# A hybrid decoder layer on one core: order of the splits ahead of the feed-forward block, place of one product in its streams, and the last pair's sums kept in SBUF

## The chip, the core and the metric

The kernel runs on one core of a Trainium2 chip. The metric is the device time in microseconds of one execution; the median of three runs is given. TensorE's clock is told by the granted clock of the profile: 1.00 is 2.4 GHz, 0.50 is 1.2 GHz.

## The reference

One decoder layer over 1024 tokens of width 1024, in float32. The part that matters here is its end:

```python
x = x + gate1 * jnp.dot(merged, w_out)
h2 = _rmsnorm(x, norm2_w) * (1.0 + scale2) + shift2
ffn = jnp.dot(jax.nn.silu(jnp.dot(h2, w_ffn_gate)) * jnp.dot(h2, w_ffn_up), w_ffn_down)
x = x + gate2 * ffn
return _rmsnorm(x, final_norm_w)
```

The hidden width of the feed-forward block is 2816, which is 22 blocks of 128 columns.

## The kernel before

**Splits.** Every factor of a matrix product is stored as two tiles, hi and lo: ScalarE copies the source into hi in a rounded format (fp32r), VectorE or GpSimd subtracts hi from the source into lo. A product is then three matmuls, hi by hi, hi by lo and lo by hi, and each is 128x512 here.

**Products.** The gate and up matrices are taken in pairs of 128-column blocks. There are 11 pairs; each pair has two streams, first gate, then up, so 22 streams. In a stream a two-by-two block product of h2 (transposed) and the weights is made out of seven products M1 to M7 with sums of blocks as factors (a Strassen-like scheme). Each product is 12 matmuls (four blocks of the contraction by three). Their sides that come from h2 lie in SBUF as "combos": h11 for M1, S1 for M5, S2 for M6, S4 for M3, S3 for M7, h21 for M2, h22 for M4. The weight sides are made new for each stream by `factor`: a difference on VectorE (L789, L795, L796), the hi on ScalarE and the lo on `lo_engine` (L750, L751), into five slots `fhi` and `flo`. M1, M6, M7 and M4 of a stream add up in one PSUM bank ("ya", four of them): after M1 and M6 ScalarE copies what is there (L807), after M7 VectorE adds it to a tile (L810), and M4 is the last in the bank. M5 and M3 share a bank of "yb" (two of them); M2 has one for itself.

**The way in.** The last stage before, x plus the gated output projection, goes tile by tile of 128 tokens in the order 4, 5, 6, 7, 0, 1, 2, 3. For each it makes the norm, transposes the normed tile on TensorE (L1377), scales the transposed blocks on ScalarE and VectorE (L1383, L1387) into `hraw`, and puts the part of the combos that this tile gives (`put_half1`, `put_half2`, `put_rest`, with `put_combo` at L1277 and L1278 for hi and lo). So the combos h11 (M1's) and h21 (M2's) are whole only when the last tile, number 3, is split. The M5 products of the first four streams need nothing of the last tiles; they stand in between, to keep TensorE busy. The rest of the combos, S2, S4 and S3, are sums and splits (`split_combo` at L1502 and L1503, sums at L1295, L1301 and L1536). Until the ninth product of the first pair VectorE makes the weights' lo halves too, afterwards GpSimd does.

**The way out.** Silu of the gate stream's four blocks (L1428) times the up stream's (L1431) gives the activations, and four sums of them follow (L1455 to L1458). Seven tiles of each pair are stored in DRAM (`act_d`, L1446). The rows of the down matrix that belong to the pair are loaded (L1473), four sums are made of them in place in one buffer `dw` (L1485), and stored in DRAM (`dw_d`, L1496). After the last pair the down projection runs in six passes (M1, M5, M6, M3, M7, M4), each over all 11 pairs, and a seventh (M2) with the final norm. Its factors are loaded again (L1583) through a ring of eight raw tiles, split (L1586 and L1587) and multiplied (L1604 to L1606).

**Order.** All instructions are written down in one order by hand, and a planner, which knows each instruction's dependencies and estimates its cost, sets from that the fixed order of each engine's queue: of what it holds ready it takes what was written first. Each engine then works its queue strictly in order. `turns_after(a, b)` tells the planner to put a behind b on the same engine without a wait at run time. DMAs all go through SyncE's queue.

Of the kernel before, what the change touches and what calls it, by code (L numbers as in the profile page):

```python
# [43 lines left out]
def tile_hybrid_layer(ctx: ExitStack, tc: tile.TileContext, x, c, w_ada, b_ada, norm1_w, w_in,  # L44
# [704 lines left out]
    def split_block(src, hi, lo, eng=None):  # L749
        ins = nc.scalar.activation(hi, src, AF.Copy)  # L750
        (eng or nc.gpsimd).tensor_sub(lo, src, f32(hi))  # L751
        return ins

    class Stream:
# [28 lines left out]
        def factor(self, m):  # L783
            b = self.blocks
            if m in ("M1", "M2", "M3"):
                src = b[{"M1": "11", "M2": "21", "M3": "22"}[m]]
            elif m == "M4":
                src = self.t2
                nc.vector.tensor_sub(src, b["21"], src)  # L789
            else:  # L790
                src = four(self.env.tmp())
                x, y = {"M5": ("12", "11"), "M6": ("22", None), "M7": ("22", "12")}[m]
                if m == "M6" and "M5" in self.early:
                    self.t1 = src
                    nc.vector.tensor_sub(src, b["12"], b["11"])  # L795
                nc.vector.tensor_sub(src, b[x], b[y] if y else self.t1)  # L796
                if m == "M5":
                    self.t1 = src
                if m == "M6":
                    self.t2 = src  # L800
            hi, lo = self.env.slot()
            self.split = split_block(src, hi, lo, self.env.lo_engine)
            return hi, lo
# [69 lines left out]
    class GateEnv:  # L873
# [20 lines left out]
        def quad(self, *_):  # L894
            self.n_q += 1
            return quads[(self.n_q - 1) % len(quads)]

        def store(self, st, dst, src):
# [376 lines left out]
    def put_combo(name, o, src):  # L1275
        hi, lo = (c[:, :, o:o + P] for c in combo[name])
        nc.scalar.activation(hi, src, AF.Copy)  # L1277
        nc.vector.tensor_sub(lo, src, f32(hi))  # L1278

# [11 lines left out]
    def put_half1(o):  # L1291

        h11, h21, h12, s1 = parts_of(o)
        put_combo("h11", o, h11)
        nc.vector.tensor_sub(s1, s1, h11)  # L1295

    def put_rest(o):

        h11, h21, h12, s2 = parts_of(o)
        put_combo("h21", o, h21)  # L1300
        nc.vector.tensor_sub(h21, h21, s2)  # L1301

    raws = []
# [27 lines left out]
    for hf in range(2):  # L1331
# [16 lines left out]
        for n, t in enumerate(order):  # L1348
# [23 lines left out]
            for g in range(2):  # L1372
# [5 lines left out]
                for i in range(4):  # L1378
# [7 lines left out]
                    else:  # L1386
                        nc.vector.tensor_scalar(h_to, h_of, sc, sh, op0=ALU.mult, op1=ALU.add)  # L1387
            (put_half2 if th else put_half1)(o)
    alloc_combo("h21")
    for i in range(4):  # L1390
        put_rest(i * P)
    st_f.close()
# [12 lines left out]
    class FfnEnv:  # L1405
        lo_engine = nc.vector

        def __init__(self):
# [38 lines left out]

    todo = []

    def finish_tasks(p):  # L1450

        g, u = streams[p, 0], streams[p, 1]
        a = g.c
        s1, s2, s3, s4 = u.c["11"], u.c["12"], u.c["22"], quad_tile("s4")
        todo.append(lambda: nc.vector.tensor_add(s1, a["21"], a["22"]))  # L1455
        todo.append(lambda: nc.vector.tensor_sub(s2, s1, a["11"]))
        todo.append(lambda: nc.vector.tensor_sub(s3, a["11"], a["21"]))
        todo.append(lambda: nc.vector.tensor_sub(s4, a["12"], s2))  # L1458
        for m, t in (("M1", a["11"]), ("M2", a["12"]), ("M4", a["22"]), ("M5", s1), ("M6", s2), ("M7", s3),
                     ("M3", s4)):  # L1460
            todo.append(lambda m=m, t=t: act_store(p, m, t))
        if p:
            down_load(p - 1)
        if p > 1:
            down_sums(p - 2)
# [13 lines left out]
    def down_sums(p):  # L1479
# [15 lines left out]
        step(b21, b21, b22)  # L1495
        todo.insert(4, lambda: nc.sync.dma_start(out=dw_d[p], in_=dws[p]))  # L1496

    def split_combo(name, srcs):
        alloc_combo(name)
        for k in range(4):  # L1500
            hi, lo = (c[:, k, :] for c in combo[name])
            nc.scalar.activation(hi, srcs[:, k, :], AF.Copy)  # L1502
            nc.vector.tensor_sub(lo, srcs[:, k, :], f32(hi))  # L1503

# [12 lines left out]
    for st in flow[:2]:  # L1517
        st.prepare("M1")
        turns_after(scaled[3], st.split)
    s3 = ffn.tile([P, 4, H], F32, name="s3", tag="dw")  # L1520
    held2 = const.tile([P, 2, H], F32, name="held2", tag="gate")

    for st, after in zip(flow, (None, {0: 2}, {2: 3}, {0: 3})):
        st.product("M5", after)
        if st.p == 0:
            turns_after(scaled[3], st.copied)
    split_combo("S2", hraw[1][:, 1])
    seq = [(st, m) for m in ("M1", "M2", "M4", "M6", "M3", "M7") for st in flow[:2]]
    n_first = len(seq)
    seq += [(st, m) for st in flow[2:] for m in ORDER if m not in st.early]  # L1530

    def behind(i):
        st, m = seq[i]
        if i == 0:
            for k in range(4):
                nc.vector.tensor_sub(s3[:, k, :], hraw[0][:, 0, k, :], hraw[1][:, 0, k, :])  # L1536
        if i == 1:
            split_combo("S4", hraw[0][:, 1])
        if i == 3:
            split_combo("S3", s3)  # L1540
        if i == 8:
            fenv.lo_engine = nc.gpsimd
        if i == 9:
            flow[2].open()
# [34 lines left out]
    def down_slot(src, lo_eng, scale=None):  # L1579
# [34 lines left out]

    ss3 = {}

    def square(t, i, c0, c1):
        if t not in ss3:
            ss3[t] = const.tile([P, 16], F32, name="ss3", bufs=4)
        sq = ffn.tile([P, H], BF16, name="sqh", tag="quad", bufs=10)  # L1620
        nc.scalar.activation(sq[:, :c1 - c0], x1[t][:, c0:c1], AF.Square, accum_out=ss3[t][:, i:i + 1])

    def final_norm(t, n_parts):
# [8 lines left out]
        nc.sync.dma_start(out=out[t * P:(t + 1) * P, H:], in_=xo[1])  # L1632
        nc.vector.scalar_tensor_tensor(xo[0], x1[t][:, :H], rs, fnorm[:, :H], op0=ALU.mult, op1=ALU.mult)
        nc.sync.dma_start(out=out[t * P:(t + 1) * P, :H], in_=xo[0])

    def second_half(t):
        square(t, 0, H, 2 * H)
        nc.gpsimd.tensor_mul(xo_all[:, (2 * t + 1) % 8, :], x1[t][:, H:], fnorm[:, H:])

# [99 lines left out]
```

## Time and profile before

| what | us |
|---|---|
| median of 3 runs (1787.62 to 1791.78) | 1787.7 |
| the profiled execution, its own time | 1787.85 |
| span in the profile, first to last instruction | 1785.9 |
| busy: TensorE, VectorE, GpSimd, ScalarE | 1701.2, 1228.8, 888.6, 754.3 |
| mean granted clock of TensorE | 0.989 |

The profile records each instruction of each engine with its start and length. A wait is the idle time of an engine ahead of an instruction, and the releaser is the instruction that ended it. Matmuls are pipelined, so that one that is listed with 0.39 us is followed by the next after some 0.23 us.

### The profile page before, as it was taken

What the parts mean: (1) busy time and instruction counts of PE and PEld (TensorE: products, weight loads), DVE (VectorE), ACT (ScalarE), POOL (GpSimd) and SP (SyncE); (2) the same over time, 40 slices, a digit from 0 to 9 for tenths busy, and PEclk for the clock granted to TensorE, in tenths of its full rate; (3) what the DMA queues carried; (4) which work ended last, traced back from release to release, by engine and by line L of the source; (5) the groups of instructions that cost most, each with busy time, mean ns of one, the idle gap of its engine ahead of it and who ended that gap; (6) DMA issues with size and microseconds to landing.
All of it is one profiled execution on the core that took longest, in us unless ns stands there. A gap on an engine that the chain in (4) does not pass through costs nothing. (4 is left out here: it accounts for less than half of the span.)

```text
span 1785.9 us, 24646 instructions
## 1 busy us (share of the span) xinstructions
PE 1701.2 (95%) x8266; PEld 1397.1 (78%) x8266; DVE 1228.8 (69%) x2089; ACT 754.3 (42%) x1469; POOL 888.6 (50%) x883
## 2 busy tenths in 40 slices
PE   5898989999989999999999999899999999999998
PEld 4797868787867888788777888688787878787887
DVE  7528789999699246469876656865656555686665
ACT  3625632342444344430477246533333333444444
POOL 4562275582665479530246640044444444556664
PEclk9999999999999999999999999999999999999999
DMA  9534552411423355865852740034445444597663
GB/s 291 147 108 144 159 161 54 148 33 51 127 77 112 116 156 186 257 203 161 193 128 72 249 162 1 30 118 159 144 151 178 147 137 147 187 311 259 212 185 109
DMA packets 182655, 266.49 MB, mean 149 GB/s; under 512 B 13872, under 2 KB 111616, under 8 KB 180096
## 3 DMA queue, kind: packets, MB, share of 16 engines
q1 hardware_dynamic: 182528, 264.91, 47.4%
q8 instruction: 65, 1.06, 0.2%
q14 instruction: 62, 0.51, 0.1%
HBM read 195.39 MB, written 69.47 MB: 148 GB/s over the span
## 5 line engine op out<-in xcount | busy, mean ns | idle before, releaser
L80 POOL TENSOR_TENSOR wlo<-wraw,whi 128x512 fp32r<-128x512 f32 (+2 forms) x116 | 144.7, 1261 | 111.4 <-ACT whi L77 101.0
L464 DVE TENSOR_SCALAR_CACHE_REDUCE eq<-score,cand 128x384 uint8<-128x384 f32 (+2 forms) x192 | 180.8, 942 | 4.5
L751 POOL TENSOR_TENSOR flo<-tmp,fhi 128x512 fp32r<-128x512 f32 x79 | 106.3, 1346 | 141.1 <-ACT fhi L750 77.0
L121 PE MATMUL mm<-whi,hT_hi 128*128 128x512 f32 (+1 forms) x432 | 160.2, 376 | 3.6 <-ACT qk L644 1.8
L123 PE MATMUL mm<-wlo,hT_hi 128*128 128x512 f32 (+1 forms) x432 | 161.5, 376 | 0.0
L124 PE MATMUL mm<-whi,hT_lo 128*128 128x512 f32 (+1 forms) x432 | 161.2, 376 | 0.0
L827 PE MATMUL ya<-hc,fhi 128*128 128x512 f32 x344 | 134.7, 392 | 2.3 <-DVE c L810 1.4
L1587 DVE TENSOR_TENSOR dslot<-draw,dslot 128x512 fp32r<-128x512 f32 x88 | 96.1, 1127 | 55.3 <-ACT dslot L1586 48.1
L829 PE MATMUL ya<-hc,fhi 128*128 128x512 f32 x344 | 134.1, 390 | 0.0
L1586 ACT ACTIVATE dslot<-draw 128x512 fp32r<-128x512 f32 x154 | 90.1, 626 | 102.1 <-DMA draw<-dw_d 22.8
L831 PE MATMUL ya<-hc,flo 128*128 128x512 f32 x344 | 132.5, 390 | 0.0
L1587 POOL TENSOR_TENSOR dslot<-draw,dslot 128x512 fp32r<-128x512 f32 x66 | 98.7, 1508 | 63.5 <-ACT dslot L1586 60.4
L751 POOL TENSOR_TENSOR flo<-raws,fhi 128x512 fp32r<-128x512 f32 x60 | 82.1, 1368 | 92.5 <-ACT fhi L750 64.3
L77 ACT ACTIVATE whi<-wraw 128x512 fp32r<-128x512 f32 (+2 forms) x116 | 67.0, 590 | 116.6 <-DMA wraw<-in_w_in_dram 48.4
L829 PE MATMUL yb<-hc,fhi 128*128 128x512 f32 x256 | 101.0, 395 | 6.1 <-DVE hc L1278 6.1
L831 PE MATMUL yb<-hc,flo 128*128 128x512 f32 x256 | 101.1, 395 | 3.2 <-POOL flo L751 3.2
L827 PE MATMUL yb<-hc,fhi 128*128 128x512 f32 x256 | 100.8, 395 | 0.6 <-DVE c L810 0.4
L750 ACT ACTIVATE fhi<-tmp 128x512 fp32r<-128x512 f32 x84 | 53.0, 631 | 113.3 <-PE ya L829 60.3
L751 POOL TENSOR_TENSOR wlo<-wraw,whi 128x512 fp32r<-128x512 f32 x52 | 80.5, 1556 | 35.1 <-ACT whi L750 33.3
L121 PEld LDWEIGHTS mm<-whi,hT_hi 128*128 128x128 f32 x432 | 81.2, 189 | 15.9 <-ACT qk L644 2.2
L1127 POOL TENSOR_SCALAR sx<-sx,mx 128x128 f32<-128x128 f32 (+7 forms) x64 | 47.5, 748 | 91.0 <-DVE mx L1126 69.4
L124 PEld LDWEIGHTS mm<-whi,hT_lo 128*128 128x128 f32 x432 | 81.7, 190 | 12.6 <-issue 0.5
(408 smaller groups left out, 4935.9 us busy)
## 6 DMA issues: line engine op xcount, KB each, us to landing
draw<-act_d SPq DMA_DIRECT2D x77, 256.0 KB
mw<-in_w_ada_dram SPq DMA_DIRECT2D x32, 512.0 KB
act_d<-c SPq DMA_DIRECT2D x64, 256.0 KB
raw<-in_w_in_dram SPq DMA_DIRECT2D x26, 512.0 KB
raws<-in_w_ffn_gate_dram SPq DMA_DIRECT2D x24, 512.0 KB
raws<-in_w_ffn_up_dram SPq DMA_DIRECT2D x24, 512.0 KB
dw<-in_w_ffn_down_dram SPq DMA_DIRECT2D x22, 512.0 KB
dw_d<-dw SPq DMA_DIRECT2D x11, 1024.0 KB
```

What stands on the lines that cost most here:

```text
L77: ins = nc.scalar.activation(hi[:, :n], raw[:, :n], AF.Copy)
L80: nc.gpsimd.tensor_sub(lo[:, :n], raw[:, :n], f32(hi[:, :n]))
L121: ins = nc.tensor.matmul(ps, lhsT=ahi, rhs=whi[:, :n], start=(i == 0), stop=False)
L123: nc.tensor.matmul(ps, lhsT=ahi, rhs=wlo[:, :n], start=False, stop=False)
L124: nc.tensor.matmul(ps, lhsT=alo, rhs=whi[:, :n], start=False, stop=(i == last))
L464: ins = [nc.vector.tensor_scalar(eq[:, :sc.shape[1]], sc, thr[j], None, op0=op, op1=ALU.add, accum_out=cnt[:, j:j + 1]) for j, sc in enume ...
L751: (eng or nc.gpsimd).tensor_sub(lo, src, f32(hi))
L827: mm = nc.tensor.matmul(ps, lhsT=whi[:, k, :], rhs=hhi[:, k, :], start=own and k == 0, stop=False, skip_group_check=True)
L829: nc.tensor.matmul(ps, lhsT=whi[:, k, :], rhs=hlo[:, k, :], start=False, stop=False, skip_group_check=True)
L831: nc.tensor.matmul(ps, lhsT=wlo[:, k, :], rhs=hhi[:, k, :], start=False, stop=k == 3, skip_group_check=True)
L1586: nc.scalar.activation(slot[:, 0], raw, AF.Copy)
L1587: lo_eng.tensor_sub(slot[:, 1], raw, f32(slot[:, 0]))
```

## The change

Three edits. First, `put_half1` and `put_rest` return the two splits of the last tile, and a new function `in_turn` puts behind them, on ScalarE and VectorE, all later weight splits, weight differences, sums and combo splits of the first products; M1's own lo halves stand ahead of h11's. One group of M5's matmuls of the fourth stream may also stand ahead of tile 3's transposes (the group that has to wait is now the second of four instead of the first). Second, from the second pair on M4 of a stream is written down behind M1 of the next stream instead of ahead of it. Third, the last pair's seven activation tiles and four sums of down rows are no longer stored and loaded again: the down passes split them from where they lie in SBUF. For that the final norm's weights, which shared a buffer with those sums, go into two tiles of their own ("quad"), and the squares of the final norm share one tile.

```diff
     def split_block(src, hi, lo, eng=None):
         ins = nc.scalar.activation(hi, src, AF.Copy)
-        (eng or nc.gpsimd).tensor_sub(lo, src, f32(hi))
-        return ins
+        return ins, (eng or nc.gpsimd).tensor_sub(lo, src, f32(hi))
...
                 if m == "M6" and "M5" in self.early:
                     self.t1 = src
-                    nc.vector.tensor_sub(src, b["12"], b["11"])
-                nc.vector.tensor_sub(src, b[x], b[y] if y else self.t1)
+                    self.env.in_turn(None, nc.vector.tensor_sub(src, b["12"], b["11"]))
+                self.env.in_turn(None, nc.vector.tensor_sub(src, b[x], b[y] if y else self.t1))
...
-            self.split = split_block(src, hi, lo, self.env.lo_engine)
+            self.split, self.lo = split_block(src, hi, lo, self.env.lo_engine)
+            self.env.in_turn(self.split, self.lo)
...
-        put_combo("h11", o, h11)
-        nc.vector.tensor_sub(s1, s1, h11)
+        ins = put_combo("h11", o, h11)
+        turns_after(nc.vector.tensor_sub(s1, s1, h11), ins[1])
+        return ins
...
-            (put_half2 if th else put_half1)(o)
+            last_h11 = (put_half2 if th else put_half1)(o)
     alloc_combo("h21")
     for i in range(4):
-        put_rest(i * P)
+        last_h21 = put_rest(i * P)
...
     class FfnEnv:
         lo_engine = nc.vector
+        behind = []
+
+        def in_turn(self, scalar, vector):
+
+            for hi, lo in self.behind:
+                if scalar is not None:
+                    turns_after(scalar, hi)
+                turns_after(vector, lo)
...
-            todo.append(lambda m=m, t=t: act_store(p, m, t))
+            if p < NP - 1:
+                todo.append(lambda m=m, t=t: act_store(p, m, t))
+            else:
+                last_act[m] = t
...
-        todo.insert(4, lambda: nc.sync.dma_start(out=dw_d[p], in_=dws[p]))
+        if p < NP - 1:
+            todo.insert(4, lambda: nc.sync.dma_start(out=dw_d[p], in_=dws[p]))
...
         turns_after(scaled[3], st.split)
+        turns_after(last_h11[1], st.lo)
+    fenv.behind = [last_h11, last_h21]
...
-    for st, after in zip(flow, (None, {0: 2}, {2: 3}, {0: 3})):
+    for st, after in zip(flow, (None, {0: 2}, {2: 3}, {1: 3})):
         st.product("M5", after)
         if st.p == 0:
             turns_after(scaled[3], st.copied)
+        else:
+            turns_after(st.copied, last_h11[0])
...
+    for i in [i for i, (st, m) in enumerate(seq[:-1]) if m == "M4" and i >= n_first]:
+        seq[i:i + 2] = seq[i + 1], seq[i]
...
-        if i == 0:
+        if i == 1:
+            fenv.behind += [(f.split, f.lo) for f in flow[:2]]
             for k in range(4):
-                nc.vector.tensor_sub(s3[:, k, :], hraw[0][:, 0, k, :], hraw[1][:, 0, k, :])
-        if i == 1:
+                fenv.in_turn(None, nc.vector.tensor_sub(s3[:, k, :], hraw[0][:, 0, k, :], hraw[1][:, 0, k, :]))
             split_combo("S4", hraw[0][:, 1])
...
-    fnorm = ffn.tile([P, 4, H], F32, name="fnorm", tag="dw")[:, 0:2, :].rearrange("p a n -> p (a n)")
-    nc.sync.dma_start(out=fnorm, in_=final_norm_w.rearrange("(o d) -> o d", o=1).partition_broadcast(P))
-    nc.gpsimd.tensor_scalar(fnorm, fnorm, float(D ** 0.5), 1.0, op0=ALU.mult, op1=ALU.mult)
+    fnorm = [quad_tile("fnorm") for _ in range(2)]
+    for hf, fn in enumerate(fnorm):
+        nc.sync.dma_start(out=fn, in_=final_norm_w[hf * H:(hf + 1) * H].rearrange("(o d) -> o d", o=1)
+                          .partition_broadcast(P))
+        nc.gpsimd.tensor_scalar(fn, fn, float(D ** 0.5), 1.0, op0=ALU.mult, op1=ALU.mult)
...
-        raw, slot = raw_ring[:, n % 8, :], slot_rings[n // 4 % 6][:, n % 4]
-        nc.sync.dma_start(out=raw, in_=src)
+        raw, slot = src if here else raw_ring[:, n % 8, :], slot_rings[n // 4 % 6][:, n % 4]
+        if not here:
+            nc.sync.dma_start(out=raw, in_=src)
...
-        s = down_slot(act_d[p][:, ACT_AT[m], :], nc.vector)
+        here = p == NP - 1
+        s = down_slot(last_act[m] if here else act_d[p][:, ACT_AT[m], :], nc.vector, here=here)
         if m in DW_AT:
+            if here:
+                return s, down_slot(dws[p][:, DW_AT[m], :], nc.gpsimd, here=True)
             src = dw_d[p][:, DW_AT[m], :]
```

## Rows read from the trace of the kernel before

**Rows 1.** The waits of TensorE from 1000 us on: who waited for whom, us, times, longest
```profile
PE yb L829 <- DVE hc L1278: 6.1, 1, 6.1
PE yb L1604 <- ACT dslot L1586: 3.3, 1, 3.3
PE yb L831 <- POOL flo L751: 3.2, 4, 0.8
PE ya L827 <- DVE c L810: 1.4, 4, 0.3
PE ty L1377 <- DVE xn L1374: 1.0, 1, 1.0
PE ya L827 <- ACT c L807: 1.0, 4, 0.2
```

**Rows 2.** Busy time by engine in the two long waits and behind each, with the granted clock
```profile
core 0: us, PE busy (x) PEld busy (x) DVE busy (x) ACT busy (x) POOL busy (x), PEclk, DMA share, GB/s
1137.00:1143.30 6.30, 0.27 (x2) 0.00 (x0) 6.30 (x12) 2.82 (x6) 0.00 (x0) 0.87 0.52 166
1143.30:1148.50 5.20, 5.16 (x12) 4.10 (x13) 5.04 (x9) 0.91 (x2) 0.00 (x0) 0.50 0.00 0
1622.90:1626.40 3.50, 0.23 (x2) 0.02 (x1) 0.00 (x0) 0.70 (x2) 1.93 (x2) 1.00 1.03 379
1626.40:1629.90 3.50, 3.50 (x9) 2.79 (x10) 2.82 (x2) 2.01 (x4) 3.49 (x3) 0.52 0.56 178
```

**Rows 3.** The timeline of VectorE around the first wait: start, length, instruction
```profile
1132.29 1.37 DVE L1387 TENSOR_SCALAR hraw<-ty,modr 128x128 f32<-128x128 f32 x4 [0.26 <-PE ty L1377]
...
1142.61 1.28 DVE L1278 TENSOR_TENSOR hc<-hraw,hc 128x512 fp32r<-128x512 f32 x2
```

**Rows 4.** Busy time by engine between the last scaling and the two splits
```profile
1133.60:1142.60 9.00, 3.67 (x17) 2.70 (x15) 9.00 (x16) 5.24 (x11) 0.00 (x0) 0.95 0.37 117
```

**Rows 5.** The timeline of ScalarE in the same stretch
```profile
1128.75 1.14 ACT L750 ACTIVATE fhi<-raws 128x512 fp32r<-128x512 f32 x2
...
1131.86 1.50 ACT L1383 ACTIVATE hraw<-ty,modr 128x128 f32<-128x128 f32 x4 [1.00 <-PE ty L1377]
...
1134.76 1.16 ACT L1277 ACTIVATE hc<-hraw 128x512 fp32r<-128x512 f32 x2
```

**Rows 6.** The timeline of TensorE ahead of the first wait
```profile
1136.20 0.61 PE L827 MATMUL yb<-hc,fhi 128*128 128x512 f32 x2
```

**Rows 7.** GpSimd by line, 1130 to 1170 us
```profile
L751 POOL TENSOR_TENSOR flo<-tmp,fhi 128x512 fp32r<-128x512 f32 x1 | 1.3, 1297 | 36.2 <-PE ya L829 36.2
```

**Rows 8.** The sums for down by the tile's view: ns, shortest, median and longest
```profile
L1485 DVE TENSOR_TENSOR dw<-dw x44: 676/693/1810, 1239.1 to 1612.3; 128x512 f32<-128x512 f32 x44
```

**Rows 9.** ScalarE's timeline at one boundary of two streams
```profile
1288.56 0.58 ACT L807 ACTIVATE c<-ya 128x512 f32<-128x512 f32 x1
...
1291.29 0.58 ACT L807 ACTIVATE c<-yb 128x512 f32<-128x512 f32 x1
```

**Rows 10.** VectorE's and TensorE's timeline at the same boundary
```profile
1290.50 0.67 DVE L810 TENSOR_TENSOR c<-c,ya 128x512 f32<-128x512 f32 x1
...
1291.23 0.50 PE L827 MATMUL ya<-hc,fhi 128*128 128x512 f32 x1 [0.35 <-DVE c L810]
```

**Rows 11.** The chain that ended last, ahead of the second wait: start, us, what
```profile
1609.13 0.69 DVE dw L1485
...
1612.29 0.70 DVE dw L1485
...
1613.01 5.80 DMA dw_d<-dw
...
1619.21 6.46 DMA draw<-dw_d
...
1625.70 0.64 ACT dslot L1586
```

More of the change, by code (lines that the diff above doesn't have):

```diff
@@ L896, in quad, with in_turn @@
             return quads[(self.n_q - 1) % len(quads)]
+        def in_turn(self, *_):
+            pass
         def store(self, st, dst, src):
@@ L1276, in put_combo @@
         hi, lo = (c[:, :, o:o + P] for c in combo[name])
-        nc.scalar.activation(hi, src, AF.Copy)
-        nc.vector.tensor_sub(lo, src, f32(hi))
+        ins = nc.scalar.activation(hi, src, AF.Copy)
+        return ins, nc.vector.tensor_sub(lo, src, f32(hi))
     def parts_of(o):
@@ L1293, in put_half1 @@
         h11, h21, h12, s1 = parts_of(o)
-        put_combo("h11", o, h11)
-        nc.vector.tensor_sub(s1, s1, h11)
+        ins = put_combo("h11", o, h11)
+        turns_after(nc.vector.tensor_sub(s1, s1, h11), ins[1])
+        return ins
     def put_rest(o):
         h11, h21, h12, s2 = parts_of(o)
-        put_combo("h21", o, h21)
+        ins = put_combo("h21", o, h21)
         nc.vector.tensor_sub(h21, h21, s2)
+        return ins
     raws = []
@@ L1448, in tile_hybrid_layer @@
     todo = []
+    last_act = {}
     def finish_tasks(p):
@@ L1501, in split_combo @@
             hi, lo = (c[:, k, :] for c in combo[name])
-            nc.scalar.activation(hi, srcs[:, k, :], AF.Copy)
-            nc.vector.tensor_sub(lo, srcs[:, k, :], f32(hi))
+            fenv.in_turn(nc.scalar.activation(hi, srcs[:, k, :], AF.Copy),
+                         nc.vector.tensor_sub(lo, srcs[:, k, :], f32(hi)))
     tmps = [tmp_tile() for _ in range(2)]
@@ L1542, in behind @@
             fenv.lo_engine = nc.gpsimd
+            fenv.behind = []
         if i == 9:
@@ L1573, in tile_hybrid_layer, with down_slot @@
     n_slot = [0]
-    fnorm = ffn.tile([P, 4, H], F32, name="fnorm", tag="dw")[:, 0:2, :].rearrange("p a n -> p (a n)")
-    nc.sync.dma_start(out=fnorm, in_=final_norm_w.rearrange("(o d) -> o d", o=1).partition_broadcast(P))
-    nc.gpsimd.tensor_scalar(fnorm, fnorm, float(D ** 0.5), 1.0, op0=ALU.mult, op1=ALU.mult)
+    fnorm = [quad_tile("fnorm") for _ in range(2)]
[3 more added lines that the diff above has]
+        nc.gpsimd.tensor_scalar(fn, fn, float(D ** 0.5), 1.0, op0=ALU.mult, op1=ALU.mult)
     xo_all = slab_tile(7, [P, 8, H], F32, "xo")
-    def down_slot(src, lo_eng, scale=None):
+    def down_slot(src, lo_eng, scale=None, here=False):
         n = n_slot[0]
         n_slot[0] += 1
-        raw, slot = raw_ring[:, n % 8, :], slot_rings[n // 4 % 6][:, n % 4]
-        nc.sync.dma_start(out=raw, in_=src)
+        raw, slot = src if here else raw_ring[:, n % 8, :], slot_rings[n // 4 % 6][:, n % 4]
+        if not here:
+            nc.sync.dma_start(out=raw, in_=src)
         if scale is not None:
@@ L1613, in add_out @@
         nc.vector.tensor_add(x1[t][:, cs], x1[t][:, cs], d)
-    ss3 = {}
+    ss3, squares = {}, []
     def square(t, i, c0, c1):
@@ L1619, in square @@
             ss3[t] = const.tile([P, 16], F32, name="ss3", bufs=4)
-        sq = ffn.tile([P, H], BF16, name="sqh", tag="quad", bufs=10)
+        if not squares:
+            squares.append(ffn.tile([P, H], BF16, name="sqh", tag="quad", bufs=10))
+        sq = squares[0]
         nc.scalar.activation(sq[:, :c1 - c0], x1[t][:, c0:c1], AF.Square, accum_out=ss3[t][:, i:i + 1])
@@ L1632, in final_norm @@
         nc.sync.dma_start(out=out[t * P:(t + 1) * P, H:], in_=xo[1])
-        nc.vector.scalar_tensor_tensor(xo[0], x1[t][:, :H], rs, fnorm[:, :H], op0=ALU.mult, op1=ALU.mult)
+        nc.vector.scalar_tensor_tensor(xo[0], x1[t][:, :H], rs, fnorm[0], op0=ALU.mult, op1=ALU.mult)
         nc.sync.dma_start(out=out[t * P:(t + 1) * P, :H], in_=xo[0])
@@ L1637, in second_half @@
         square(t, 0, H, 2 * H)
-        nc.gpsimd.tensor_mul(xo_all[:, (2 * t + 1) % 8, :], x1[t][:, H:], fnorm[:, H:])
+        nc.gpsimd.tensor_mul(xo_all[:, (2 * t + 1) % 8, :], x1[t][:, H:], fnorm[1])
     banks = {"A": [ps_a() for _ in range(4)], "B": [ps_b(), ps_b(), ps_ty(), ps_ty()]}
```

## The prediction

> **What bounds the kernel now.** I read the page first: TensorE is busy 1701.2 of 1785.9 us, so what can be won is where TensorE waits, and what its clock loses behind a wait. Then I read its waits from 1000 us on, where all three edits lie [rows 1]. They are of three kinds. One long wait, 6.1 us, for a lo half of a combo (L1278). One of 3.3 us, in the down passes, for a split (L1586). And twelve short ones in the streams: four for GpSimd's lo half (3.2 us together), four for VectorE's add (1.4 us), four for ScalarE's copy (1.0 us). The windows on the long waits [rows 2] show a second cost: behind the first the granted clock is 0.50 for 5.2 us, behind the second 0.52 for 3.5 us, so that matmuls take twice as long there; elsewhere around them it is 1.00.
>
> Who is to blame for the first wait is seen on VectorE. The last scaling of tile 3 begins at 1132.29 and lasts to 1133.66, and the two lo halves that TensorE waits for begin only at 1142.61 [rows 3]. ScalarE had the two hi halves ready at 1135.92 (1134.76 plus 1.16) [rows 5]. In between VectorE is busy all 9.0 us, with 16 instructions in the window of which the first is the scaling's end [rows 4]; the other 15 are weight differences, sums and weight lo halves for later products. So it is a matter of order alone.
>
> The second wait is read from the chain of work that ended last [rows 11]: the last pair's four sums on VectorE (1609.13 to 1612.99), their store to DRAM (5.80 us), the load of one of them back (6.46 us), its split on ScalarE at 1625.70, then TensorE.
>
> **The splits first.** The change puts 13 of the 15 instructions behind the two lo halves; the other two are M1's own lo halves, which must stay ahead. Each takes 9.0 / 15 = 0.60 us from start to start [rows 4]. Latest case: VectorE ends the scaling at 1133.66, makes M1's two lo halves to 1134.9 (their hi halves are ready from 1129.89 [rows 5]), then h11's to 1135.5 and h21's to 1136.1. ScalarE ends its scaling at 1133.36 [rows 5] and can give h11's hi half at about 1134.0 (0.58 us, half of the 1.16 for two), h21's at 1134.5, both before VectorE asks. TensorE is busy with M5 until 1136.20, where in this trace it begins the products of h11 and h21 [rows 6]. So both halves come just in time, M5 being the cover. The wait of 6.1 us goes, and with it the slow clock behind it: twelve matmuls in the 5.2 us window [rows 2] took 0.43 us apiece instead of 0.23, which makes 2.4 us. Term: -8.5 us. Bounds: -7.0 (h11's lo half 1.5 us late, as two or three instructions more in front of it would make it) and -8.7 (half of the 5.2 us instead of 2.4).
>
> The group of M5 that may go ahead of the transposes can fill part of the 1.0 us that TensorE waits there for the normed tile [rows 1]: three matmuls of 0.23 us, 0.7 us at most, nothing if the queue stays as it is, and it ends the cover earlier by as much. Term: -0.3.
>
> Then the 13 instructions come later, and what is late next is what they feed: M6's and M4's weight factors, S2, S4 and S3. TensorE goes through M1 and M2 of both streams first, 48 matmuls at 0.23 us, 10.9 us, to about 1147.1. Until then VectorE, at 0.60 us apiece from 1136.1, can make 18 instructions: the weight lo halves of M2 (two), the differences (four), S2's last sum and four lo halves, M6's first lo half, that is 12, so that six others may come between. From there each product gives it 2.7 us, or four to five instructions, and needs two to four. It is enough, with 2 to 4 us to spare, but the queue is a planner's. Term: +1.0; bounds 0 and +4 (half of the 13 x 0.60 = 7.8 us).
>
> **M4 behind the next M1.** At a boundary of two streams, ScalarE has copied the next stream's M1 ("c<-ya") at 1288.56 [rows 9], and M4 of the stream before begins at 1291.23, when VectorE's add to the tile of M7 has been made at 1290.50 [rows 10]. So in TensorE's queue M4 already stands behind the next M1, even behind its M5: the planner had found nothing else ready. Writing it down so changes the queue little. What it can move is who comes first to a free slot or tile: M1's factor and copy then go ahead of M4's. Four of the short waits are M6 waiting for just that copy. The bounds are the short waits: all of them, 5.6 us idle and 0.1 us to start again for each of 12 (a first matmul of 0.50 us instead of 0.39 [rows 10]), 6.8 us won; or as much again lost, if the new order brings as many more. I take a value nearer to nothing: -1.5.
>
> **The last pair on chip.** Store and load go away, 12.3 us of the chain [rows 11]; what remains is sums, split on ScalarE (0.64 us) and GpSimd's lo half (1.3 us as in [rows 7]). If VectorE ends the sums at 1612.99 as before, the factor is there at about 1615, and TensorE needs it at 1622.9 [rows 2]. So the wait of 3.3 us goes, and the slow clock behind it: 3.5 us at 0.52 are 1.7 us lost. The load that sat in this raw tile also held the next load for the same tile; that one comes earlier, too, and with eleven tiles fewer to load the transfers have room, at a DMA share of 1.03 in the wait [rows 2]. Term: -5.0; bounds -5.0 and -3.0 (the next factor 2 us late). Seven stores less cost TensorE nothing now, since it waited for no DMA directly in the streams. The final norm's weights are now two scalings on GpSimd that may sit in front of a lo half if their loads come late: +0.3, bounds 0 and +2.
>
> **The sum.** It is made against the profiled execution's 1787.85 us (span 1785.9 and 1.95 around it; 0.15 above the median, so I make no correction). 1787.85 - 8.5 - 0.3 + 1.0 - 1.5 - 5.0 + 0.3 = 1773.85, that is 1773.9 us, 0.8% faster. What a measurement of this kernel can tell from no change is about 0.3%, 5.4 us.
>
> **Rivals.**
>
> *The moved work comes back as a wait.* If the queue puts sums for M3 and M7 ahead of what M6 and M4 need, TensorE waits there for VectorE instead. For it: VectorE has been busy 9.0 of 9.0 us, and all of that is still to be done; against it: the count above. Price 4 us, 1777.5. It gets worse if the moved instructions slip behind the end of GpSimd's rest of 36.2 us, which ends ahead of 1170 [rows 7]. The same kind of subtraction takes 0.68 us alone and up to 1.81 us at its longest [rows 8]; 13 at 1.1 us more are 14 us, and nothing is left of the first edit: 1787. On this the Trainium skill, "SBUF — State Buffer", section "Who interferes with whom", says that a VectorE instruction with two SBUF inputs and a GpSimd one that reads SBUF exclude each other for a whole instruction; the spread in the row agrees with that. Chance 0.14.
>
> *M4's new place makes a wait in each stream; this one is slower than before.* M4's factor now gets its slot behind M1's; if M4 stays where it is in TensorE's queue, its lo half on GpSimd may come too late in every stream. The price of one is a short wait for GpSimd, 0.8 us [rows 1] and 0.1 to start again, 0.9 us. With 20 streams that is 18 us, instead of the 1.5 that I count as won: 1773.9 + 1.5 + 18 = 1793.4. It eats the whole gain of the other terms, 12.5 us, from 0.63 us a stream on. Against it: TensorE reaches M4 two products after M1, 5.5 us, and ScalarE and GpSimd take 2 us for a factor. Chance 0.06.
>
> *The down wait stays.* The sums, not the transfers, would then be late: their load begins only when the buffer's former sums are stored, and the four sums sit in VectorE's queue among splits. If they ended 10 us later, at 1623, the wait would be what it is: 1773.9 + 5.0 = 1779. Or another factor is late at the same place. Chance 0.12.
>
> *Two of these together*: 1783 to 1786. Chance 0.08.
>
> **How the numbers follow.** The forecast, 1773.9 with a range of its own from 1769 to 1778, has 0.60. Faster by over 0.3% (below 1782.3) are the forecast, nearly all of the first rival and the third: 0.84. Within 0.3%: 0.10, the pairs and the bad end of the first rival. Slower by over 0.3%: 0.06, the second rival. The range for 8 in 10 goes down to 1768.0 (the short waits won as well, with 1.0 left out) and up to 1782.0, which leaves the pairs and the slow rival outside.
>
> **What would show it.** Right: no wait for L1278 around 1136 us and a clock of 1.00 there; VectorE's two L1278 directly behind the last L1387 and at most two L751; no transfers of `dw_d` and `act_d` for the last pair, and no wait for L1586 between M5 and M6 of the down passes. Wrong: a new wait of TensorE for L751, L1503 or L789 in the 30 us behind 1136; a short wait that repeats in every stream instead of every fourth; a wait at about 1620 for VectorE or a DMA.

## The result and the profile after

The changed kernel takes 1773.57 us (median of 4 runs, 1771.72 to 1774.9); the kernel before, beside it, 1787.66 us (1785.36 to 1791.78). The ratio is 0.9918, 95% interval 0.9898 to 0.9938, that is 14.7 us less on 1787.7 (11.1 to 18.2); the two medians differ by 14.1. The forecast was 1773.9 us. The total is right, but two terms of the sum are far off, and their errors point in opposite directions.

The profiled execution takes 1774.9 us (span 1773.1, mean clock 0.990). TensorE's waits from 1000 us on, beside [rows 1]: the 6.1 us, the 3.3 us, the 1.0 us ahead of the transposes, and all but one of the short waits are gone. Four others stand in the list: 1.9 and 1.8 us, which belong to one product, 1.6 us (in the first line, with the short wait that is left) and 0.6 us.

```profile
PE ya L827 <- DVE c L810: 2.0, 2, 1.6
PE ya L831 <- DVE flo L751: 1.9, 1, 1.9
PE ya L827 <- ACT fhi L750: 1.8, 1, 1.8
PE ya L829 <- DVE hc L1281: 0.6, 1, 0.6
```

The windows of the changed kernel, in the columns of [rows 2]: the first combos, the new double wait, the stretch behind it, and the place of the former wait in the down passes.

```profile
1136.00:1142.30 6.30, 5.72 (x25) 4.31 (x24) 6.27 (x13) 6.30 (x15) 0.00 (x0) 1.00 0.01 3
1150.60:1155.80 5.20, 1.49 (x6) 0.63 (x5) 5.20 (x10) 5.02 (x9) 0.00 (x0) 1.00 0.26 88
1155.80:1159.60 3.80, 3.80 (x11) 2.94 (x11) 3.80 (x7) 2.33 (x5) 0.00 (x0) 0.55 0.18 69
1612.00:1620.00 8.00, 8.00 (x37) 6.60 (x36) 4.72 (x4) 5.69 (x11) 5.12 (x4) 1.00 0.87 306
```

Where the first wait was, TensorE now makes 25 matmuls in 6.3 us at a clock of 1.00. But eight microseconds behind that window it makes six in 5.2 us, and then the clock is 0.55 for 3.8 us: a smaller copy of what [rows 2] show.

VectorE's timeline in the changed kernel answers to [rows 3]. The last scaling (L1392) is followed by one sum, M1's two lo halves and then the two combo halves (L1281), 3.1 us behind the scaling's start and no longer 10.3.

```profile
1135.93 1.37 DVE L1392 TENSOR_SCALAR hraw<-ty,modr 128x128 f32<-128x128 f32 x4
1137.21 0.68 DVE L1305 TENSOR_TENSOR hraw<-hraw,hraw 128x512 f32<-128x512 f32 x1
1137.81 1.29 DVE L751 TENSOR_TENSOR flo<-raws,fhi 128x512 fp32r<-128x512 f32 x2
1139.01 1.29 DVE L1281 TENSOR_TENSOR hc<-hraw,hc 128x512 fp32r<-128x512 f32 x2
...
1142.75 2.49 DVE L1562 TENSOR_TENSOR s<-hraw,hraw 128x512 f32<-128x512 f32 x4
...
1149.97 1.29 DVE L795 TENSOR_TENSOR tmp<-raws,tmp 128x512 f32<-128x512 f32 x2
1151.18 1.28 DVE L810 TENSOR_TENSOR c<-c,yb 128x512 f32<-128x512 f32 x2
1152.38 2.49 DVE L1521 TENSOR_TENSOR hc<-hraw,hc 128x512 fp32r<-128x512 f32 x4
1154.78 0.69 DVE L751 TENSOR_TENSOR flo<-tmp,fhi 128x512 fp32r<-128x512 f32 x1
```

The last line is the lo half of M6 of the first pair. TensorE's timeline says what it was worth: the two bracketed waits end with ScalarE's hi half and with this lo half.

```profile
1150.69 0.39 PE L831 MATMUL yb<-hc,flo 128*128 128x512 f32 x1
1152.86 0.50 PE L827 MATMUL ya<-hc,fhi 128*128 128x512 f32 x1 [1.78 <-ACT fhi L750]
1153.19 0.40 PE L829 MATMUL ya<-hc,fhi 128*128 128x512 f32 x1
1155.52 0.55 PE L831 MATMUL ya<-hc,flo 128*128 128x512 f32 x1 [1.94 <-DVE flo L751]
```

The hi half is late for a reason of ScalarE's own queue: S4's four hi halves (L1520) stand ahead of it.

```profile
1150.09 2.19 ACT L1520 ACTIVATE hc<-hraw 128x512 fp32r<-128x512 f32 x4 [3.82 <-DVE hc L1521]
1152.19 0.61 ACT L750 ACTIVATE fhi<-tmp 128x512 fp32r<-128x512 f32 x1
```

The boundary of [rows 10] is the one where a short wait is left in the streams, and it is the same 0.35 us:

```profile
1290.60 0.50 PE L827 MATMUL ya<-hc,fhi 128*128 128x512 f32 x1 [0.35 <-DVE c L810]
```

In the chain that ended last, [rows 11] have no counterpart: from 1570 to 1640 us it consists of matmuls of the down passes alone.

**A table by stretches.** The queues of both kernels are the same up to the last normed tiles, yet the changed kernel's profiled execution reaches the first scaling of a normed tile (VectorE, L1374 before) at 1085.37 us and the one before at 1081.25. Over all executions profiled here this time lies between 1080.2 and 1085.4 with nothing changed ahead of it, which is a part of the spread of the totals. So the table counts from there. Each column is the time from one matmul of TensorE's queue to another, from the timelines: I to the last matmul of M2 of the first pair, II the next 172 (the rest of the first pair, mostly), III the next 1400 (the streams), IV the next 200 (end of the streams), V the next 800 (down passes), VI the rest. Each of these profiles lists 8266 matmuls.

| kernel | I | II | III | IV | V | VI | sum |
|---|---|---|---|---|---|---|---|
| before | 74.40 | 39.01 | 326.61 | 47.05 | 186.71 | 30.91 | 704.69 |
| changed | 65.31 | 44.88 | 317.98 | 47.25 | 181.37 | 30.95 | 687.75 |
| e1 splits alone | 65.32 | 45.09 | 326.77 | 47.11 | 187.89 | 30.92 | 703.11 |
| e2 M4 alone | 73.81 | 38.99 | 317.99 | 47.25 | 181.96 | 30.93 | 690.94 |
| e3 on chip alone | 74.65 | 38.99 | 326.67 | 47.06 | 182.66 | 31.57 | 701.59 |
| e4 all but M4 | 65.30 | 44.81 | 326.63 | 47.05 | 182.75 | 31.58 | 698.12 |
| e5 all but splits | 74.15 | 38.99 | 318.02 | 47.26 | 181.38 | 30.95 | 690.75 |
| e6 all but on chip | 65.31 | 45.09 | 318.02 | 47.26 | 182.48 | 30.92 | 689.08 |
| e7 M6 first | 65.31 | 40.33 | 317.33 | 47.25 | 181.36 | 30.94 | 682.52 |
| e8 and add first | 65.31 | 40.33 | 317.33 | 46.10 | 181.73 | 30.94 | 681.75 |
| e9 eleven tiles | 73.97 | 38.99 | 326.70 | 47.09 | 182.33 | 30.92 | 699.99 |
| e10 factors alone | 73.83 | 38.99 | 321.29 | 47.09 | 184.43 | 30.92 | 696.54 |
| e11 products alone | 74.11 | 38.99 | 318.00 | 47.25 | 181.87 | 31.23 | 691.44 |
| e12 M5 group back | 64.62 | 44.77 | 318.00 | 47.25 | 181.35 | 30.95 | 686.94 |

From before to changed: -9.1, +5.9, -8.6, +0.2, -5.3, 0.0, in all -16.9 us; the later start takes 4.1 of it back in this pair of executions (1785.9 to 1773.1). Where two kernels have the same TensorE queue in a column from I to IV, the numbers agree within 0.3 us (I of the kernels with the old way in: within 0.9), so there the table resolves what the medians can't. V is not so steady. In the four kernels with the old queue there (before, e1, e9, e10) it lies between 182.3 and 187.9 us, and the wait for the split in it between 0.4 and 3.4 us; in the ten others V lies between 181.3 and 182.8. In VI only e3, e4 and e11 stand out, by 0.3 to 0.7 us.

### The profile page after: what moved, and what is told of

It is laid out like the page before. It is cut to its first block, busy times and chain, and to the rows that moved or that the text cites. A ratio compares the mean times of both kernels' runs of the same rounds, so it can differ in the third digit from the quotient of the medians.

```text
span 1773.1 us, 24644 instructions
## 1 busy us (share of the span) xinstructions
PE 1696.8 (96%) x8266; PEld 1396.7 (79%) x8266; DVE 1235.2 (70%) x2089; ACT 753.9 (43%) x1469; POOL 897.0 (51%) x884
## 4 chain that ended last, share of the span: by engine, by line
PE 71%; DVE 18%; DMA 4%; issue 3%; POOL 2%; ACT 2%; SPq 0%; POOLq 0%; DVEq 0%; ACTq 0%
DVE eq L464 6%; PE ya L827 4%; PE ya L831 4%; PE ya L829 4%; PE yb L827 3%; PE yb L831 3%; PE yb L829 3%; PE pva L1162 3%; PE ya L1639 2%; PE ya L1637 2%; PE ya L1638 2%; PE tra L1141 2%; PE mm L121 2%; PE mm L123 2%; PE mm L124 2%
## 5 line engine op out<-in xcount | busy, mean ns | idle before, releaser
L751 POOL TENSOR_TENSOR flo<-tmp,fhi 128x512 fp32r<-128x512 f32 x79 | 107.8, 1365 | 145.7 <-ACT fhi L750 103.7
L1616 ACT ACTIVATE dslot<-draw 128x512 fp32r<-128x512 f32 x143 | 84.4, 627 | 94.7 <-DMA draw<-act_d 20.8
L751 POOL TENSOR_TENSOR flo<-raws,fhi 128x512 fp32r<-128x512 f32 x60 | 86.2, 1443 | 74.6 <-ACT fhi L750 36.3
L1617 DVE TENSOR_TENSOR dslot<-draw,dslot 128x512 fp32r<-128x512 f32 x81 | 88.7, 1128 | 47.1 <-ACT dslot L1616 47.0
L751 POOL TENSOR_TENSOR wlo<-wraw,whi 128x512 fp32r<-128x512 f32 x52 | 80.4, 1554 | 35.1 <-ACT whi L750 33.3
```

What stands on the lines that cost most here:

```text
L751: return ins, (eng or nc.gpsimd).tensor_sub(lo, src, f32(hi))
L1616: nc.scalar.activation(slot[:, 0], raw, AF.Copy)
L1617: lo_eng.tensor_sub(slot[:, 1], raw, f32(slot[:, 0]))
```

## The experiments

Each was timed in five rounds beside the kernel before; a ratio is to that, with its 95% interval, and the microseconds behind it are the ratio's on 1787.7.

**The edits one by one**: e1 has the splits and the M5 group, e2 the exchange in `seq`, e3 the last pair on chip, e4 the first and third.

```diff
 # e1, on the kernel before
+    fenv.behind = [last_h11, last_h21]
...
 # e2, on the kernel before
+    for i in [i for i, (st, m) in enumerate(seq[:-1]) if m == "M4" and i >= n_first]:
+        seq[i:i + 2] = seq[i + 1], seq[i]
 # e3, on the kernel before
+            if p < NP - 1:
+                todo.append(lambda m=m, t=t: act_store(p, m, t))
+            else:
+                last_act[m] = t
...
 # e4, on the changed kernel
-    for i in [i for i, (st, m) in enumerate(seq[:-1]) if m == "M4" and i >= n_first]:
-        seq[i:i + 2] = seq[i + 1], seq[i]
```

> The first edit alone (splits of the last normed tile first, and the M5 group). Theory A (the first wait goes, but VectorE's sums and S4's splits then stand ahead of M6's factors): -9.0 us at the way in, +5.8 us given back at M6 of the first pair, in all about -3.2 us, 1784.5 us beside 1787.7; the short waits of the streams stay, twelve or so. Theory B (the prediction's sum: -8.5 -0.3 +1.0): 1779.9 us. Theory C (the short waits vanish because the streams start from another state): -3.2 and -9 more, 1775.5 us.

Measured: 1784.84 us, ratio 0.9992 (0.9981 to 1.0003), 1.4 us less (from 3.4 less to 0.5 more). Theory A, with the table: column I -9.1, column II +6.1, column III as before. It can hardly be told from no change.

> The second edit alone (M4 written behind the next stream's M1). Theory A (the new order takes away the short waits of the streams): 8 to 10 us less, 1778 to 1780 us, no short waits between 1205 and 1550 us; the new wait of 1.6 us at the last stream's M4 comes with it. Theory B (the prediction's sum): -1.5 us, 1786.2 us. Theory C (the short waits go only with edit 1): no change, 1787.7 us. The slow rival of the prediction: up to 18 us more.

Measured: 1775.65 us, ratio 0.9937 (0.9923 to 0.9951), 11.3 us less (8.8 to 13.8). Theory A, and more: one short wait is left in the streams, and the wait in the down passes is gone as well, which no theory had. From 1000 us on its list holds the 6.1 us of the first combo, the 1.0 us ahead of the transposes, and the adds' 2.0 us in two, as in the changed kernel.

In the streams the gain is larger than the short waits add up to. Busy time from 1205 to 1550 us, before and then with M4 alone:

```profile
1205.00:1550.00 345.00, 339.63 (x1479) 276.07 (x1477) 205.56 (x225) 123.29 (x211) 165.71 (x123) 1.00 0.45 153
```

```profile
1205.00:1550.00 345.00, 344.65 (x1521) 285.05 (x1520) 213.04 (x230) 128.29 (x223) 178.93 (x128) 1.00 0.46 159
```

TensorE is idle 5.4 us in the first, yet makes 42 matmuls fewer, at 0.227 us 9.5 us of work. A matmul is listed with 0.39 us and the next begins 0.23 us behind it, so 0.16 us of each halt is listed as busy; the first matmul behind it is listed with 0.50 us, and the next begins 0.34 us behind it and not 0.23. A short wait of 0.24 us in the list cost 0.24 + 0.16 + 0.11 = 0.51 us, and halts of under 0.16 us don't stand in the list at all.

> The third edit alone (last pair's activations and sums stay in SBUF). Theory A and the prediction's sum: the wait of 3.3 us in the down passes and the slow clock behind it go, 5 us less, 1782.7 us. Rival (the wait moves to another factor of the down passes, or the final norm's scalings make one): under 3 us less, over 1784.7 us.

Measured: 1782.97 us, ratio 0.9975 (0.9964 to 0.9985), 4.5 us less (2.7 to 6.4). Theory A within its error; column V gives 4.1 us, VI takes 0.7 back, and a wait of 1.0 us for VectorE's product of gate and up (L1431) is new.

> All of the change but the second edit. Theory A (the second edit takes away the short waits): 1787.7 - 3.2 - 5.2 = 1779.3 us, with the short waits back between 1205 and 1550 us. Theory B (the prediction's sum, second edit worth 1.5 us): 1775.1 us. Theory C (the streams' short waits go with edit 1): 1774 us, few short waits.

Measured: 1782.7 us, ratio 0.9973 (0.9962 to 0.9984), 4.8 us less (2.9 to 6.8). The short waits are all back (column III 326.6). Theory A is nearer than B, but the kernel is slower than it said: the second edit is worth 14.7 - 4.8 = 9.9 us in the company of the others, not 1779.3 - 1773.6 = 5.7.

**Which edits overlap.** e5 is e2 with the third edit, e6 is e1 with the second.

```diff
 # e5, on the changed kernel: the first edit's lines as before
-    for st, after in zip(flow, (None, {0: 2}, {2: 3}, {1: 3})):
+    for st, after in zip(flow, (None, {0: 2}, {2: 3}, {0: 3})):
...
 # e6, on the changed kernel: the third edit's lines as before
-            if p < NP - 1:
-                todo.append(lambda m=m, t=t: act_store(p, m, t))
-            else:
-                last_act[m] = t
+            todo.append(lambda m=m, t=t: act_store(p, m, t))
```

> Second and third edit without the first. Theory A (with the second edit the last pair's sums come early enough for the down passes by themselves, so the third edit has nothing left to take away): 1775.6 us, as the second edit alone. Theory B (the third edit takes its 4.6 us away whatever the order of the streams): 1771 us. In both the first wait of 6.1 us stays.

Measured: 1774.6 us, ratio 0.9935 (0.9922 to 0.9949), beside 0.9937 for the second edit alone. Theory A.

> First and second edit without the third: store and load of the last pair stay. Theory A (as above): 1773.6 us, as the whole change, and no wait for a split of the down passes near 1610 to 1625 us. Theory B: 1778.2 us, with a wait of about 3.3 us there.

Measured: 1772.71 us, ratio 0.9917 (0.9902 to 0.9932), beside 0.9918 for the whole change. Theory A: once the second edit is in, the third has almost nothing left (column V -1.1 us, with a wait of 0.4 us that it removes). Why is seen on VectorE: with the second edit alone the last four sums begin at 1597.48, where they began at 1609.13 [rows 11].

```profile
1597.48 3.84 DVE L1485 TENSOR_TENSOR dw<-dw 128x512 f32<-128x512 f32 x4
```

That is 11.7 us earlier, while the matmuls of column V begin only 8.4 us earlier (1081.91 + 478.04 = 1559.95 beside 1081.25 + 487.07 = 1568.32). The 3.3 us between them are the wait [rows 1]; store and load need no shortening. Counted from the first matmul of column V, the sums begin at 40.8 us before and at 37.5 us in e2. In e9, with VectorE's queue as before, they begin at 37.1 us, and the wait is down to 0.4 us there: the wait goes with the time of the sums, and the second edit is not the only thing that moves it.

**The wait given back at M6.** e7 puts the sums for S3 and S4's splits behind M6's factors of the first pair; e8 also puts VectorE's lo halves of the down passes behind the add of the last M7.

```diff
 # e7, on the changed kernel
+            self.splits[m] = self.split, self.lo
...
-        if i == 1:
-            fenv.behind += [(f.split, f.lo) for f in flow[:2]]
+        if i == 3:
+            fenv.behind += [f.splits[x] for f in flow[:2] for x in ("M2", "M6")]
...
-        if i == 3:
+        if i == 5:
             split_combo("S3", s3)
 # e8, on e7
-        lo_eng.tensor_sub(slot[:, 1], raw, f32(slot[:, 0]))
+        ins = lo_eng.tensor_sub(slot[:, 1], raw, f32(slot[:, 0]))
+        if lo_eng is nc.vector and n >= 8:
+            turns_after(ins, flow[-1].adds["22"])
```

> The whole change, and the sums for S3 and S4's splits written down two products later and put behind the splits of M2 and M6 of the first pair, S3's splits two products later too. Theory A (the two waits of 1.8 and 1.9 us at M6 of the first pair, and the slow clock behind them, come from those instructions standing ahead of M6's factors): 5 to 6 us less than the changed kernel, 1768 us, without those two waits and with a clock of 1.00 there. Rival (S2's lo halves or the weights' loads are late anyway): 0 to 2 us less, 1772 to 1774 us. Rival (S4 or S3 now come late themselves): a new wait at M3 or M7, 1773 us or more.

Measured: 1766.74 us, ratio 0.9888 (0.9872 to 0.9905), 20.0 us less than before (17.0 to 22.9), and so 5.3 us less than the changed kernel. Theory A. Both waits are gone, and VectorE's timeline in this kernel shows why: between the combo halves (L1282) and M6's lo half (the last L751 line shown) stand 12 instructions, where the changed kernel had 24.

```profile
1138.39 1.29 DVE L1282 TENSOR_TENSOR hc<-hraw,hc 128x512 fp32r<-128x512 f32 x2
...
1142.01 1.29 DVE L751 TENSOR_TENSOR flo<-raws,fhi 128x512 fp32r<-128x512 f32 x2
...
1146.83 0.69 DVE L751 TENSOR_TENSOR flo<-tmp,fhi 128x512 fp32r<-128x512 f32 x1
...
1150.15 2.49 DVE L1563 TENSOR_TENSOR s<-hraw,hraw 128x512 f32<-128x512 f32 x4
```

The clock stays at 1.00 in the windows where it had been 0.55:

```profile
1155.80:1159.60 3.80, 3.80 (x19) 3.14 (x18) 3.80 (x7) 3.12 (x7) 0.40 (x1) 1.00 0.76 257
```

A wait of 1.0 us for GpSimd's lo half is new, and with it column II stays 1.3 us above that of before.

> As the kernel with M6's factors first, and VectorE's lo halves of the down passes, from the ninth factor on, put behind the add of the last stream's M7. Theory A (the new wait of 1.6 us at the last stream's M4 is VectorE's queue order): another 1.5 to 1.9 us less, 1766.3 us. Rival (the lo halves held back come late in the down passes): no gain, 1768 us or more.

Measured: 1763.96 us, ratio 0.9872 (0.9857 to 0.9887), 22.9 us less than before (20.2 to 25.6); in the table 0.8 us less than e7, about half of what was expected, since 0.5 us of the wait stays and column V is 0.4 us longer. It beats both kernels. What held up the add is seen on VectorE, and then on GpSimd, in the changed kernel:

```profile
1552.09 0.68 DVE L810 TENSOR_TENSOR c<-c,yb 128x512 f32<-128x512 f32 x1
...
1553.80 1.78 DVE L1617 TENSOR_TENSOR dslot<-draw,dslot 128x512 fp32r<-128x512 f32 x1
1555.51 1.78 DVE L1444 TENSOR_TENSOR c<-c,c 128x512 f32<-128x512 f32 x1
1557.21 1.77 DVE L1617 TENSOR_TENSOR dslot<-draw,dslot 128x512 fp32r<-128x512 f32 x1
1558.90 0.68 DVE L1502 TENSOR_TENSOR dw<-dw 128x512 f32<-128x512 f32 x1
1559.50 0.67 DVE L810 TENSOR_TENSOR c<-c,ya 128x512 f32<-128x512 f32 x1
```

```profile
1551.90 6.53 POOL L1617 TENSOR_TENSOR dslot<-draw,dslot 128x512 fp32r<-128x512 f32 x4 [1.49 <-ACT dslot L1616]
```

Three instructions of 1.78 us stood ahead of the add that M4 waited for, all three beside GpSimd's work; alone they take 0.68. An earlier add with one source in PSUM (yb, at 1552.09) took 0.68 us beside the same work of GpSimd. The rule that the prediction named from the Trainium skill, "SBUF — State Buffer", section "Who interferes with whom", says both: a VectorE instruction with two SBUF inputs contends with a GpSimd instruction that reads SBUF, and one with at most one SBUF input, outside VectorE's two-port modes, does not. The rows agree.

**What the second edit does.** e9 gives the kernel before an eleventh quad tile; e10 makes the exchange for the factors alone, e11 for the products alone.

```diff
 # e9, on the kernel before
-        return ffn.tile([P, H], F32, name=name, tag="quad", bufs=10)
+        return ffn.tile([P, H], F32, name=name, tag="quad", bufs=11)
 # e10, on the kernel before: factors in the exchanged order, products in the old one
-    run(seq, 2, behind)
+    run(seq, 2, behind, made=swapped)
 # e11: the other way round
+    seq, swapped = swapped, seq
+    run(seq, 2, behind, made=swapped)
```

> The kernel before with eleven quad tiles instead of ten (the room comes from fewer buffers of two small tiles of the final norm), M4 where it was. Theory T (a part of the streams' short waits comes from the tile that M1's copy gets, which an activation store still holds): M6's waits for ScalarE's copy (1.0 us in four) go, and with them what they cost again, 2 to 4 us less, 1784 to 1786 us; the waits for GpSimd's lo half (3.2 us in four) stay. Rival S (only the order of the instructions counts, tiles are free in time): 1787.6 us, all short waits as before.

Measured: 1787.56 us, ratio 1.0001 (0.9985 to 1.0018). Rival S: all short waits stay, column III is unchanged. TensorE's queue in it is the same as before, instruction by instruction. In its profiled execution the wait in the down passes is 0.4 us and not 3.3 (column V 182.3), but the timed runs show no such gain. With the same TensorE queue in V the wait is 3.4 us in e1 and 2.6 in e10; what makes it differ from one execution to another is open.

> The second edit on the kernel before, for the factors only: M1's splits of the next stream are written ahead of M4's of this one, the products keep their old order. Theory A (the slot order makes GpSimd's lo half late): the waits for GpSimd's lo half (3.2 us in four, about 4.3 us of time) go, 1783 us; M6's waits for ScalarE's copy stay. Rival (the products' order does everything): 1787.6 us.

Measured: 1780.97 us, ratio 0.9971 (0.9957 to 0.9984), 5.2 us less (2.9 to 7.7). The size is theory A's, the waits are not: GpSimd's four are all left, though shorter (1.6 us together, three of them under 0.3), and the four for ScalarE's copy are gone, which theory A left in place. So this split does not separate two causes.

> The other half of the second edit on the kernel before: M1 of the next stream, with its copy, is written ahead of M4 of this one, while the splits keep their old order. Theory A (two causes): M6's waits for ScalarE's copy go, and most of VectorE's, 4 to 5 us less, 1783 us; the waits for GpSimd's lo half stay. Rival (the products' order does everything): 1776 us, no short waits. Rival (the slots do everything): 1787.6 us.

Measured: 1773.93 us, ratio 0.9927 (0.9906 to 0.9948), 13.1 us less (9.3 to 16.8); column III is 318.0, as in the whole change. The rival holds: the products' order alone is enough for all of it. It is not the only way to a gain, since the factors' order alone took 5.3 of the 8.6 us in column III (e10).

What that order does at one boundary is read from ScalarE's timeline, before and then changed:

```profile
1273.07 0.63 ACT L750 ACTIVATE fhi<-raws 128x512 fp32r<-128x512 f32 x1 [4.29 <-PE ya L829]
1273.61 0.58 ACT L1428 ACTIVATE c<-ya 128x512 f32<-128x512 f32 x1
1274.08 0.59 ACT L807 ACTIVATE c<-ya 128x512 f32<-128x512 f32 x1
```

```profile
1268.90 0.58 ACT L807 ACTIVATE c<-ya 128x512 f32<-128x512 f32 x1
1273.35 0.63 ACT L750 ACTIVATE fhi<-raws 128x512 fp32r<-128x512 f32 x1 [3.87 <-PE ya L829]
1273.88 0.58 ACT L1441 ACTIVATE c<-ya 128x512 f32<-128x512 f32 x1
```

Before, the copy of the next stream's M1 (L807) stands behind the Silu of M4's block (L1428), and so waits until M4 is through, though its own product has long been made; M6 of that stream waits for the copy. Afterwards the copy is written ahead of the Silu and runs 5 us ahead of it. In e9 the copy still stands behind the Silu (1274.23 and 1274.71), and the wait is the same. But in e10 it stands there too, and the wait is gone:

```profile
1269.41 0.58 ACT L1429 ACTIVATE c<-ya 128x512 f32<-128x512 f32 x1
1269.89 0.59 ACT L807 ACTIVATE c<-ya 128x512 f32<-128x512 f32 x1
```

There TensorE makes M4 ahead of the next stream's M5, not behind most of it, and begins M6 only at 1272.24. By this the copy's place behind the Silu costs something only where M4 comes shortly ahead of M6. And the four waits for the copy are a part of the gain only: at the 0.51 us apiece that was read at e2 they are 2.0 of the 8.6 us. For the waits for GpSimd and VectorE, which make up most of the rest, no cause is shown.

**The M5 group.**

```diff
 # e12, on the changed kernel
-    for st, after in zip(flow, (None, {0: 2}, {2: 3}, {1: 3})):
+    for st, after in zip(flow, (None, {0: 2}, {2: 3}, {0: 3})):
```

> The whole change with the M5 group back where it was (the first of the four groups waits for tile 3's transposes, not the second). The prediction's term: 0.3 us more than the changed kernel, 1773.9 us, at most 0.7; the wait of 1.0 us ahead of tile 3's transposes comes back, and the wait of 0.6 us for the lo half of h11 goes or shrinks. Rival (the cover counts, not the wait): 0.3 us less.

Measured: 1770.74 us, ratio 0.9909 (0.9889 to 0.9929); column I is 64.62, 0.7 us less than in the changed kernel, and the wait of 0.6 us for h11's lo half is gone. The wait of 1.0 us ahead of the transposes does not come back. The medians can't tell 0.7 us, the column can: the rival holds.

## Why the prediction was right in total and wrong in two terms

- **The first wait (-8.5) and the M5 group (-0.3)**: column I gives -9.1 beside -8.8 (-8.5 to -9.3, by which of the seven kernels with the old way in is taken). The mechanism is as told: order alone, the halves behind the scaling, a clock of 1.00; 0.6 us of wait for h11's lo half is left. The small term had the wrong sign: the group taken ahead costs 0.7 us, since the cover ends earlier (e12), and the 1.0 us ahead of the transposes went with the splits' order, not with the group. So the splits are worth about 9.8.
- **The moved instructions (+1.0, bounds 0 and +4)**: this step failed, column II gives +5.9. The count was that twelve instructions, M6's first lo half the last of them, stand behind the combo halves, and that there is time for six others, 18 in all. In the queue there were 24 ahead of that lo half, 25 with it: S3's four sums, S4's four lo halves, the two adds behind M2, two more differences and one sum (L1298) had been put in. Seven more than there was time for, at 0.60 us apiece, are 4.2 us; the two waits are 3.7. The step counted VectorE's queue alone; the first of the two waits ended with a hi half that stood behind S4's on ScalarE. It is the first rival, with its mechanism (sums for M3 and M7 ahead of what M6 needs), given 0.14; its price of 4 us left out the slow clock, eight matmuls at 0.43 instead of 0.23 us, 1.6 us. A wait of TensorE for L751 within 30 us was also the first sign that the prediction named for being wrong. e7 shows the cause: the same instructions two products later, and 4.6 of the 5.9 us come back in column II.
- **M4 (-1.5, bounds 6.8 either way)**: this step failed too. Column III gives -8.6, beyond the bound. The reading of TensorE's queue was sound, M4 already stood behind the next M1; but from that the step took it that little would change, and looked for an effect in free slots and tiles alone. What the runs show in its place is that the order in which the products are written is worth all 8.6 us (e11); one part, about 2.0 us, is read from ScalarE's queue, where M1's copy stood behind M4's Silu. The tiles are refuted by e9; the slots are not, since the factors' order alone gives 5.3 us (e10). Why VectorE's and GpSimd's short waits go was not taken apart further, and stays open: e10 and e11 each change the queues of all engines. The bound was too small because it added 0.1 us to each listed wait, where the rows show 0.27 (0.16 and 0.11, as read at e2) and halts that are not listed, and because [rows 1] leave out a thirteenth short wait, 0.4 us for VectorE's add. The new 1.6 us at the last stream's M4 shows as only +0.2 in column IV, since it takes the place of a wait for the add and one for GpSimd that stood there before (0.34 and 0.79 us in the list).
- **The last pair on chip (-5.0)**: column V gives -5.3, near the term, but with the second edit in little of it is this edit's doing. With the second edit alone V goes from 186.71 to 181.96 (e2), and the third adds 1.1 at most (e6 to changed). How much of the 4.7 us is the second edit's can't be read from one execution, since V before is not steady (e9 has 182.33); the timed runs bear it out that the two overlap: the third edit takes 4.5 us alone (e3), and beside the second nothing that can be measured (e5 to e2, e6 to changed). Alone it does what the step says. The step treated two edits as independent that remove the same wait.
- **The final norm (+0.3)**: column VI gives 0.0 (with the third edit and not the second, e3 and e4, 0.7).

The errors are +4.9 and -7.1, and the others are under 0.5: the sum of the six columns is -16.9 beside a forecast of -14.0, and the ratio's interval of 11.1 to 18.2 us holds both. That the median came out within 0.4 us of the forecast is luck: two errors cancelled for the most part, and the term for the last pair was met in part by another edit. The slow rival, M4's factors late in every stream, did not occur in any kernel.

## What to carry to other kernels

An order that lets one wait go moves work, and the price is read by writing down the queue that will stand ahead of the next consumer, instruction by instruction; here eleven were counted ahead of it and 24 stood there. Price a short halt by what TensorE did not do (matmuls per stretch), not by its listed idle time. And where two edits are said to remove waits that lie behind one another, time each without the other: here one of three was worth 4.5 us alone and nothing measurable beside the second.

## What the runs showed of the hardware

- TensorE's listed idle time understates halts: 5.4 us idle in 345 us went with 9.5 us of missing matmuls. The Trainium skill, "Perfetto Trace Analysis", section "Tensor Engine Instruction (MATMUL, LD_WEIGHTS)", says that the end of a matmul in the trace is an estimate; the listed 0.39 us beside a start-to-start of 0.23 us agrees.
- Two waits of 1.78 and 1.94 us with two matmuls between them were followed by a granted clock of 0.55 for 3.8 us. One wait of 1.64 us (ahead of the matmul at 1560.23) was not: the window behind it reads 1.00. In the down passes a wait of 3.4 us was followed by 0.50 (e1, 1624.2 to 1627.7), and one of 2.6 us by 1.00 (e10, 1619.4 to 1622.9).

```profile
1560.20:1564.00 3.80, 3.77 (x16) 3.11 (x17) 3.80 (x5) 1.79 (x3) 1.41 (x2) 1.00 0.99 358
```

- Executions whose queues are the same up to that point reached the first normed tile anywhere between 1080.2 and 1085.4 us, while behind it the same TensorE queue took the same time within 0.3 us a column, but for the columns I, V and VI as told with the table. Where the 5 us arise was not looked into.
